# A hybrid S5 and HGRN2 block on one core: the framework orders three engines by another machine model, and two raw weight tiles change their pool

## The chip, the cores and the metric

The kernel runs on one core of one Trainium2 chip. The metric is the device time of one execution in microseconds, as a median of three runs. A profiled execution has a time of its own; its span, from the first to the last instruction on the engines, is a little shorter. The engines are TensorE (PE in the profile's rows; PEld is its loading of weights), VectorE (DVE), ScalarE (ACT) and GpSimd (POOL). SyncE (SP) computes nothing here and issues most of the DMAs; ScalarE issues some too.

## The reference

The block takes x (2048 tokens of width 1024, float32), normalises it, projects it to nine pieces, sends them through two causal token mixers, merges the two with gates, projects once more, adds x and normalises again. Cut to what matters:

```python
xn = rms_norm(h, norm_w)
proj = xn @ w_in                                   # 1024 -> 5632
u_a, z_a, q_b, f_b, i_b, og_b, z_b, g_a, g_b = split(proj)
y_a = s5_branch(u_a, z_a, ...)                     # diagonal complex state space, GELU, GLU, gate
y_b = hgrn2_branch(q_b, f_b, i_b, og_b, z_b, ...)  # gated linear recurrence, head norm, gate
merged = sigmoid(g_a) * (y_a @ w_proj_a) + sigmoid(g_b) * (y_b @ w_proj_b)
out = rms_norm(h + merged @ w_out, final_norm_w)
```

## The kernel before

**Tiling.** The sequence is cut into two halves of 1024 tokens (index `a` in names), each half into two blocks of 512 (index `b`). All products have 512 columns and use operands split into a high and a low part in the format fp32r: `split` (lines 118 to 120) copies the high part on ScalarE (L119) and subtracts on VectorE to get the low part (L120), and each product is three matmuls, high by high, high by low, low by high. The input projection is cut into 22 slices of 256 output columns. The first slices (u, the first q/f and the first i/og) are multiplied plainly for the first half (`plain`, L355 to L357). All others go through `strassen` (L458 to L460), which forms seven products in place of eight; the sums of the results are ScalarE copies and VectorE additions (L464, L467), and the weight operands come from `w_ops`.

**Weights.** For the first half `w_ops` loads a slice's raw weights (L383), splits them, forms the seven operands and stores them to DRAM (L391, tensors `wc`). For the second half it reads them back (L375). Four slices of the second half were plain in the first: numbers 0 and 1 (u), 2 (the first q/f, `SL_QF`) and 6 (the first i/og, `SL_VO`). For these the raw weights are loaded once more. Which pool they go to is what line 382 decides: `y4` has two buffers of 128x1024, `wr4` has three.

**The mixers.** The HGRN2 core (`hgrn_block`) runs nine levels of score products (L959 to L991, tiles `sc`), each with VectorE updates of Q and K between them (L1016, L1017), then the state (L1029, L1038) and the output. Its root mean square is the accumulated square of L1054, a Newton iteration on VectorE (L155 to L161, tile `rso`), a scaled ScalarE copy (L1077, tile `ys`) and a transpose on TensorE (L1081). The S5 core (`ssm_batch`) has VectorE work around three products (L791, L829, L830). `norm_stats` loads x (L186, L190, tiles `xr`) and accumulates its squares on ScalarE (L187, L191); `norm_diag` and `norm_bcast` turn them into factors by way of one product with ones (L205). `x_load` reads the transformed second half of x back (L287, tiles `xq`, also from the pool `y4`) and splits it into the tiles `X1..`, which names write as X103h for half 1, row block 0, operand 3, high part.

**What sets the order.** TensorE's order is written by hand: the whole body stands in a block in which the order of the code is TensorE's, and lists of timed events (`heads`, `steps`, `timed`) place the mixers' steps between the matmuls of the projection. The order of the other engines and of the DMA queues is not the code's. The framework's scheduler walks the program with a model of the machine, and whenever an engine is free in that model it gives it, among the instructions that are ready in the model, the one that stands first in the code. Each engine then runs its list strictly in that order on the chip, and a tile's buffer is given out in that order too. The lines that matter here:

```python
yp = ctx.enter_context(tc.tile_pool(name="yp", bufs=2))          # y4
wpool = ctx.enter_context(tc.tile_pool(name="wpool", bufs=3))    # wr4
...
raw = (y4 if a and sl != SL_VO else wr4)(f"rw{n}_{kh}")...
...
with tc.manual_schedule(engines={mybir.EngineType.PE}):
...
with tile.TileContext(nc) as tc:
```

Of the kernel before, what the change touches and what calls it, by code (L numbers as in the profile page):

```python
# [27 lines left out]
SL_U, SL_QF, SL_VO, SL_ZB, SL_ZA, SL_GA, SL_GB = 0, 2, 6, 10, 12, 14, 18  # L28
# [3 lines left out]
def hybrid_block(  # L32
# [24 lines left out]
    nc = tc.nc  # L57
# [48 lines left out]
    def wo4(name):  # L106
        return wpool.tile([128, 1024], F32R, name=name, tag="wo", bufs=5)
# [10 lines left out]
    def split(raw, hi, lo):  # L118
        S.activation(hi, raw, AF.Copy)  # L119
        V.tensor_tensor(lo, raw, hi.bitcast(F32), op=ALU.subtract)  # L120
# [249 lines left out]
    def w_ops(a, sl):  # L370
        n = f"{a}_{sl}"
        if sl in wc_d:
            for p in range(7):
                t = wo4(f"w{n}_{p}")
                nc.sync.dma_start(t.bitcast(F32), wc_d[sl][p])  # L375
                yield t
            return
        if a == 0:
            wc_d[sl] = [dram.tile([128, 1024], F32, name=f"wc{sl}_{p}") for p in range(7)]

        def get(kh):
            raw = (y4 if a and sl != SL_VO else wr4)(f"rw{n}_{kh}").rearrange("p (k n) -> p k n", k=4)
            nc.sync.dma_start(raw, wi[sl, kh])  # L383
            return raw[:, :, 0:128], raw[:, :, 128:256]

        def op(p, raw):
            t = wo4(f"w{n}_{p}")
            v = t.rearrange("p (i k n) -> p i k n", i=2, k=4)
            split(raw, v[:, 0], v[:, 1])
            if a == 0:  # L390
                nc.sync.dma_start(wc_d[sl][p], t.bitcast(F32))  # L391
            return t

        a11, a21 = get(0)
        yield op(0, a11)
        a12, a22 = get(1)
        s1 = wpool.tile([128, 4, 128], F32, name=f"s1{n}", tag="wt", bufs=2)
        s2_ = wpool.tile([128, 4, 128], F32, name=f"s2{n}", tag="wt", bufs=2)
        t = op(1, a12)
        V.tensor_tensor(s1, a21, a22, op=ALU.add)  # L400
        yield t
        V.tensor_tensor(s2_, a11, s1, op=ALU.subtract)
        yield op(2, s2_)
        t = op(3, s1)
        V.tensor_tensor(a11, a11, a21, op=ALU.subtract)
        yield t
        t = op(4, a11)
        V.tensor_tensor(a12, a12, s2_, op=ALU.add)
        yield t
        yield op(5, a22)  # L410
        yield op(6, a12)
# [1232 lines left out]
```

## Time and profile before

| | us |
|---|---|
| median of three runs (1541.31 to 1543.61) | 1541.35 |
| the profiled execution | 1540.05 |
| its span | 1538.3 |
| TensorE busy | 1467.0 |
| TensorE loading weights | 1207.3 |
| VectorE busy | 1100.8 |
| ScalarE busy | 637.6 |
| TensorE's waits of over 0.2 us, together | 63 |

Busy times overlap between engines, so they do not add up. TensorE is busy 95% of the span. The granted clock stands at full speed nearly throughout; ten short stretches are at half speed, the last of them at the end.

### The profile page before, as it was taken

What the parts mean: (1) busy time and instruction counts of PE and PEld (TensorE: products, weight loads), DVE (VectorE), ACT (ScalarE), POOL (GpSimd) and SP (SyncE); (2) the same over time, 40 slices, a digit from 0 to 9 for tenths busy, and PEclk for the clock granted to TensorE, in tenths of its full rate; (3) what the DMA queues carried; (4) which work ended last, traced back from release to release, by engine and by line L of the source; (5) the groups of instructions that cost most, each with busy time, mean ns of one, the idle gap of its engine ahead of it and who ended that gap; (6) DMA issues with size and microseconds to landing.
All of it is one profiled execution on the core that took longest, in us unless ns stands there. A gap on an engine that the chain in (4) does not pass through costs nothing.

```text
span 1538.3 us, 21386 instructions
## 1 busy us (share of the span) xinstructions
PE 1467.0 (95%) x7360; PEld 1207.3 (78%) x7360; DVE 1100.8 (72%) x2409; ACT 637.6 (41%) x1391; POOL 3.6 (0%) x24
## 2 busy tenths in 40 slices
PE   7997999999999999999989999999989899899997
PEld 5776788788888777878878887788878688688886
DVE  5798688678678659956665887776649877765445
ACT  7456454454454634323323455333353332532222
POOL 0000000000000000000000000000000000000000
PEclk9998999999999999999999999999999999999999
DMA  9539778977977883786668559677977854854602
GB/s 336 175 115 305 284 278 295 316 255 269 331 264 286 285 271 119 186 245 197 231 201 313 174 163 294 217 259 264 327 236 234 266 184 137 274 171 131 212 14 103
DMA packets 192060, 354.53 MB, mean 230 GB/s; under 512 B 65680, under 2 KB 74896, under 8 KB 191952
## 3 DMA queue, kind: packets, MB, share of 16 engines
q1 hardware_dynamic: 163792, 328.00, 63.6%
q10 hardware_dynamic: 28160, 25.17, 4.8%
q8 instruction: 58, 0.95, 0.3%
q14 instruction: 50, 0.41, 0.1%
HBM read 214.17 MB, written 138.94 MB: 230 GB/s over the span
## 4 chain that ended last, share of the span: by engine, by line
PE 68%; DVE 15%; DMA 10%; ACT 3%; issue 3%; SPq 0%; ACTq 0%; DVEq 0%
PE pd L458 14%; PE pd L460 13%; PE pd L459 13%; PE pf L1284 3%; PE pf L1285 3%; PE pf L1286 3%; PE pp L1112 2%; PE pp L1111 2%; PE pp L1110 2%; PE sc L979 2%; DMA y_d<-T 1%; DVE w L120 1%; DMA xb<-in_xt_dram 1%; DMA xq<-xo_d 1%; PE pd L355 1%
## 5 line engine op out<-in xcount | busy, mean ns | idle before, releaser
L119 ACT ACTIVATE w<-rw 128x512 fp32r<-128x512 f32 x110 | 68.7, 628 | 112.7 <-PE pd L460 67.9
L1284 PE MATMUL pf<-ho,mh 128*128 128x512 f32 x256 | 101.2, 395 | 5.2 <-ACT mh L119 5.2
L1286 PE MATMUL pf<-ho,ml 128*128 128x512 f32 x256 | 100.6, 393 | 0.5 <-DVE ml L120 0.5
L1285 PE MATMUL pf<-lo,mh 128*128 128x512 f32 x256 | 100.3, 392 | 0.0
L464 ACT ACTIVATE u<-pd 128x512 f32<-128x512 f32 x80 | 47.5, 594 | 106.0 <-PE pd L460 103.3
L120 DVE TENSOR_TENSOR w<-rw,w 128x512 fp32r<-128x512 f32 x110 | 75.3, 685 | 16.9 <-ACT w L119 16.6
L467 DVE TENSOR_TENSOR u<-u,pd 128x512 f32<-128x512 f32 x80 | 54.8, 685 | 33.5 <-PE pd L460 22.8
L355 PE MATMUL pd<-xh,hw 128*128 128x512 f32 x128 | 52.4, 409 | 9.0 <-ACT hw L119 6.7
L1284 PEld LDWEIGHTS pf<-ho,mh 128*128 128x128 f32 x256 | 48.6, 190 | 15.4 <-ACT mh L119 5.5
L1286 PEld LDWEIGHTS pf<-ho,ml 128*128 128x128 f32 x256 | 48.4, 189 | 11.6 <-DVE ml L120 1.6
L1285 PEld LDWEIGHTS pf<-lo,mh 128*128 128x128 f32 x256 | 48.6, 190 | 9.9
L119 ACT ACTIVATE mh<-sgl 128x512 fp32r<-128x512 f32 x32 | 20.0, 629 | 86.7 <-DVE sgl L1227 86.3
L356 PE MATMUL pd<-xl,hw 128*128 128x512 f32 x128 | 51.2, 400 | 0.0
L357 PE MATMUL pd<-xh,lw 128*128 128x512 f32 x128 | 50.9, 397 | 0.0
L980 DVE COPY_PREDICATED s_buf<-masks,sc 128x256 f32<-128x256 uint8 x64 | 32.5, 508 | 25.0 <-PE sc L979 25.0
L1110 PE MATMUL pp<-yh,hpa 128*128 128x512 f32 x128 | 50.2, 392 | 0.0
L1112 PE MATMUL pp<-yh,lpa 128*128 128x512 f32 x128 | 49.9, 390 | 0.2 <-DVE lpa L120 0.2
L1111 PE MATMUL pp<-yl,hpa 128*128 128x512 f32 x128 | 50.0, 390 | 0.0
L1226 DVE TENSOR_TENSOR sgl<-sgl,pp 128x512 f32<-128x512 f32 x48 | 32.7, 683 | 23.0 <-PE pp L1112 22.9
L1016 DVE TENSOR_TENSOR Q<-Q,t 128x256 f32<-128x256 f32 x96 | 40.5, 422 | 10.0 <-PE sc L991 9.9
L974 ACT ACTIVATE KX<-K 128x128 f32<-128x128 f32 x128 | 32.6, 304 | 35.6 <-DVE K L1017 26.3
L979 PEld LDWEIGHTS sc<-Q,KX 128*128 128x128 f32 x256 | 38.0, 189 | 8.9 <-issue 1.8
(915 smaller groups left out, 4431.6 us busy)
## 6 DMA issues: line engine op xcount, KB each, us to landing
wc<-w SPq DMA_DIRECT2D x126, 512.0 KB, 3.4
w<-wc SPq DMA_DIRECT2D x126, 512.0 KB, 4.6
rw<-in_wi_dram SPq DMA_DIRECT2D x44, 512.0 KB, 4.6
sgl<-sg_d SPq DMA_DIRECT2D x48, 256.0 KB, 3.2
sg_d<-u ACTq DMA_DIRECT2D x32, 256.0 KB, 3.5
ro<-in_wo_dram SPq DMA_DIRECT2D x16, 512.0 KB, 5.1
hh<-in_xn_dram SPq DMA_DIRECT2D x32, 256.0 KB, 5.1
out_dram<-hh SPq DMA_DIRECT2D x32, 256.0 KB, 2.4
```

The lines of the kernel that those rows point to most:

```text
L119: S.activation(hi, raw, AF.Copy)
L120: V.tensor_tensor(lo, raw, hi.bitcast(F32), op=ALU.subtract)
L458: mm(o, w[:, 0, k], xh, start=(first and k == 0), stop=False, skip_group_check=True)
L459: mm(o, w[:, 0, k], xl, start=False, stop=False, skip_group_check=True)
L460: mm(o, w[:, 1, k], xh, start=False, stop=(k == 3), skip_group_check=True)
L979: mm(ps[:, :, c, :], ch(kx, c), qp, start=True, stop=True)
L1110: mm(ps, hi[:, k, fs], yh, start=(k == 0), stop=False)
L1111: mm(ps, hi[:, k, fs], yl, start=False, stop=False)
L1112: mm(ps, lo[:, k, fs], yh, start=False, stop=(k == last))
L1284: mm(o, mh[:, ts_], hi, start=(kk == 0), stop=False)
L1285: mm(o, mh[:, ts_], lo, start=False, stop=False)
L1286: mm(o, ml[:, ts_], hi, start=False, stop=(kk == 7))
```

## The change

Two edits. The scheduler is told to use its timeline model in place of the default one while it orders VectorE, ScalarE and the queues. And the raw weights of slice 2 of the second half, which is the first slice of that half, are loaded into `wr4` and no longer into `y4`; slices 0 and 1 stay in `y4`, slice 6 stays in `wr4`.

```diff
-            raw = (y4 if a and sl != SL_VO else wr4)(f"rw{n}_{kh}").rearrange("p (k n) -> p k n", k=4)
+            raw = (y4 if a and sl < SL_QF else wr4)(f"rw{n}_{kh}").rearrange("p (k n) -> p k n", k=4)
...
-    with tile.TileContext(nc) as tc:
+    with tile.TileContext(nc, schedule_with_timeline_sim=True) as tc:
```

No instruction is added or removed. TensorE's list is the same, row for row. VectorE's list of some 2300 rows differs from end to end, ScalarE's and SyncE's lists in most stretches. Three places are shown; the names carry the tile's indices.

ScalarE in the first half, while slice 10 (the first z slice) is multiplied. `u20_10` and `u30_10` are copies of a product out of `pd0_10_0`, after which TensorE may write that bank again; `xr..` are loads of x for the second half's norm, squared here. Before:

```order
L191 ACTIVATE xr102_1268,ssx_237<-xr102_1268 128x1024
L191 ACTIVATE xr103_1271,ssx_237<-xr103_1271 128x1024
L974 ACTIVATE KX001_1357<-K001_1355 128x64x2 x2
L464 ACTIVATE u20_10_1316<-pd0_10_0_1224 128x512
L191 ACTIVATE xr110_1505,ssx_237<-xr110_1505 128x1024
L191 ACTIVATE xr111_1508,ssx_237<-xr111_1508 128x1024
L464 ACTIVATE u30_10_1391<-pd0_10_0_1224 128x512
```

The same place in the changed kernel:

```order
L191 ACTIVATE xr102_1268,ssx_237<-xr102_1268 128x1024
L119 ACTIVATE w0_14_1_1413<-rw0_14_1_1409 128x512
L191 ACTIVATE xr103_1271,ssx_237<-xr103_1271 128x1024
L191 ACTIVATE xr110_1505,ssx_237<-xr110_1505 128x1024
L464 ACTIVATE u20_10_1316<-pd0_10_0_1224 128x512
L191 ACTIVATE xr111_1508,ssx_237<-xr111_1508 128x1024
L191 ACTIVATE xr112_1511,ssx_237<-xr112_1511 128x1024
L191 ACTIVATE xr113_1514,ssx_237<-xr113_1514 128x1024
L464 ACTIVATE u30_10_1391<-pd0_10_0_1224 128x512
```

One square has moved ahead of `u20_10`, and two more ahead of `u30_10`.

ScalarE at the end of the first half's projection. `ys030` is the scaled copy that the transpose L1081 reads, `Y031h` the high part of the last head's output, which `merge_b` multiplies (L1110, L1111); the tiles X1.. are splits of loads by `x_load`. Before:

```order
L1077 ACTIVATE ys030_5298<-O030_4557,rso_240 128x128 x4
L1077 ACTIVATE ys031_5343<-O031_4512,rso_240 128x128 x4
L119 ACTIVATE Y030h_5325<-zy030_4987 128x512
L119 ACTIVATE X132h_5453<-xq21_5391 128x512
L119 ACTIVATE X103h_5476<-xq30_5419 128x512
L119 ACTIVATE X113h_5501<-xq30_5419 128x512
L119 ACTIVATE Y031h_5370<-zy031_4989 128x512
L119 ACTIVATE X123h_5526<-xq31_5457 128x512
L119 ACTIVATE X133h_5549<-xq31_5457 128x512
L119 ACTIVATE X104h_5572<-xq40_5505 128x512
```

The same place in the changed kernel:

```order
L119 ACTIVATE X103h_5476<-xq30_5419 128x512
L1077 ACTIVATE ys030_5298<-O030_4557,rso_240 128x128 x4
L1077 ACTIVATE ys031_5343<-O031_4512,rso_240 128x128 x4
L119 ACTIVATE X113h_5501<-xq30_5419 128x512
L119 ACTIVATE Y030h_5325<-zy030_4987 128x512
L119 ACTIVATE X123h_5526<-xq31_5457 128x512
L119 ACTIVATE X133h_5549<-xq31_5457 128x512
L119 ACTIVATE X104h_5572<-xq40_5505 128x512
L119 ACTIVATE Y031h_5370<-zy031_4989 128x512
```

The split X103h, which needs the load xq30, has moved ahead of `ys030`; three splits of the loads xq31 and xq40 have moved ahead of `Y031h`.

SyncE's queue in the second half, where slice 15's stored operand 4 (`w1_15_4`, L375) is read back among the loads for the first S5 batch (WU00, VM00, E0). Before:

```order
L375 DMA w1_15_3_7557<-wc15_3_2410 128x1024
L863 DMA zb_d1_2_176<-ezb121_7572 128x512
L758 DMA WU00_7585<-w_d_87 128x512
L759 DMA WU00_7585<-u_d0_0_92 128x512
L760 DMA VM00_7586<-v_d_88 128x512
L761 DMA VM00_7586<-m_d_89 128x512
L767 DMA E0_7594<-el_d_90 128x4x32
L768 DMA E0_7594<-eh_d_91 128x4x16
L375 DMA w1_15_4_7597<-wc15_4_2411 128x1024
```

The same place in the changed kernel:

```order
L375 DMA w1_15_3_7557<-wc15_3_2410 128x1024
L767 DMA E0_7594<-el_d_90 128x4x32
L768 DMA E0_7594<-eh_d_91 128x4x16
L375 DMA w1_15_4_7597<-wc15_4_2411 128x1024
L383 DMA rw1_0_0_8321<-in_wi_dram 128x1024
L863 DMA zb_d1_3_177<-ezb130_7534 128x512
L375 DMA w1_19_0_7654<-wc19_0_2653 128x1024
L782 DMA cs_d0_108<-CC00_7591 128x512
L375 DMA w1_15_5_7681<-wc15_5_2412 128x1024
```

The read of operand 4 now stands ahead of four loads of the S5 batch and of the store that it followed.

## Rows read from the trace of the kernel before

**Rows 1.** The page: the span, and TensorE's busy time, its share and its instructions.

```profile
span 1538.3 us, 21386 instructions
PE 1467.0 (95%) x7360; PEld 1207.3 (78%) x7360; DVE 1100.8 (72%) x2409; ACT 637.6 (41%) x1391; POOL 3.6 (0%) x24
```

**Rows 2.** What TensorE waited for, longest first: the waiting line, what ended the wait, then us in total, times, the longest. The view has 22 such rows, from the first to the last shown here; a row for the first weights (6.7 us at the start of the program) is among those left out.

```profile
PE pd L458 <- ACT u L464: 13.4, 4, 6.6
...
PE pg L1110 <- ACT gh L119: 6.7, 2, 3.9
...
PE pf L1284 <- ACT mh L119: 5.2, 1, 5.2
PE pd L458 <- DMA w<-wc: 4.5, 2, 2.6
PE sc L967 <- DVE kl L120: 4.5, 1, 4.5
PE pv L1029 <- DVE st L1038: 3.4, 2, 2.0
...
PE sc L979 <- DVE Q L1016: 2.2, 2, 1.4
...
PE pp L1112 <- DVE lpa L120: 0.2, 1, 0.2
```

**Rows 3.** The start. One row of busy times by stretch (us from:to, length, busy us and count of TensorE, weight loads, VectorE, ScalarE, GpSimd, then granted clock, DMA share, GB/s), then rows of the timeline (start us, us, engine, line, operation, count): the loads of x for the first norm, the last square, the last step of the factors, and the two products with ones.

```profile
0.00:38.00 38.00, 28.97 (x110) 22.49 (x111) 21.45 (x46) 27.57 (x55) 2.04 (x10) 1.00 0.95 337
```

```profile
13.95 5.06 SPq L186 DMA_DIRECT2D xr<-in_xn_dram  x8
24.10 0.63 ACT L187 ACTIVATE xr<-xr 128x512 f32<-128x512 f32 x1
30.21 0.88 DVE L200 TENSOR_SCALAR dg<-ident,rst 128x128 f32<-128x128 f32 x4
31.85 1.02 PE L205 MATMUL psn<-dg,ones 128*128 128x512 f32 x2
55.70 1.13 PE L205 MATMUL psn<-dg,ones 128*128 128x512 f32 x2 [1.03 <-DVE dg L200]
```

**Rows 4.** The timeline of ScalarE and TensorE around the first place shown above: `u20_10` (L464), the squares of xr110 and xr113 (L191), and the two matmuls that write over what `u20_10` and `u30_10` copied; then the time from issue to landing of the eight loads of these tiles.

```profile
130.69 0.57 ACT L464 ACTIVATE u<-pd 128x512 f32<-128x512 f32 x1
134.24 1.06 ACT L191 ACTIVATE xr<-xr 128x1024 f32<-128x1024 f32 x1 [2.97 <-DMA xr<-in_xn_dram]
141.31 1.05 ACT L191 ACTIVATE xr<-xr 128x1024 f32<-128x1024 f32 x1
131.32 0.80 PE L458 MATMUL pd<-X004h,w 128*128 128x512 f32 x1 [6.60 <-ACT u L464]
139.28 0.39 PE L458 MATMUL pd<-X005h,w 128*128 128x512 f32 x1
DMA to landing us min/median/max: 3.8/4.7/7.3
```

**Rows 5.** The timeline near 230 us: the VectorE addition that makes `u30_7`, the first two scalings of the next block of x, and the transpose that reads `u30_7`.

```profile
229.49 0.68 DVE L467 TENSOR_TENSOR u<-u,pd 128x512 f32<-128x512 f32 x1
236.90 1.41 DVE L248 SCALAR_TENSOR_TENSOR xa<-xa,nw_t,rb 128x512 f32<-128x512 f32 x2 [0.77 <-DMA xa<-in_xt_dram]
230.89 0.60 PE L911 MATMUL pt<-ident,u 128*128 128x128 f32 x4
```

**Rows 6.** The timeline around the second place: `ys030` and `ys031`, X103h, `Y031h`, X104h on ScalarE, and the matmul that reads the low part of `Y031`.

```profile
540.33 2.43 ACT L1077 ACTIVATE ys<-O,rso 128x128 f32<-128x128 f32 x8
543.93 0.62 ACT L119 ACTIVATE X103h<-xq 128x512 fp32r<-128x512 f32 x1
548.86 0.63 ACT L119 ACTIVATE Y031h<-zy 128x512 fp32r<-128x512 f32 x1 [3.79 <-DVE zy L1082]
550.44 0.61 ACT L119 ACTIVATE X104h<-xq 128x512 fp32r<-128x512 f32 x1
550.88 0.50 PE L1111 MATMUL pb<-Y031l,hpb 128*128 128x512 f32 x1 [0.84 <-DVE Y031l L120]
```

**Rows 7.** SyncE's queue at the third place: the last load of the S5 batch ahead of operand 4, and the read of operand 4 (L375).

```profile
784.03 0.59 SPq L768 DMA_DIRECT2D E<-eh_d  x1
786.56 0.33 SPq L375 DMA_DIRECT2D w<-wc  x1
```

**Rows 8.** The price of one VectorE operation on 128x512 (the costliest group of the page: busy us, mean ns), and the timeline near 1109 us: the last Newton step of `rso`, the copy `ys130` that needs it, and the transpose that needs the copy.

```profile
L120 DVE TENSOR_TENSOR w<-rw,w 128x512 fp32r<-128x512 f32 x110 | 75.3, 685 | 16.9 <-ACT w L119 16.6
```

```profile
1108.42 0.17 DVE L161 SCALAR_TENSOR_TENSOR rso<-small,rso 128x8 f32<-128x8 f32 x1
1108.67 1.28 ACT L1077 ACTIVATE ys<-O,rso 128x128 f32<-128x128 f32 x4 [0.40 <-DVE rso L161]
1109.12 0.33 PE L1081 MATMUL py<-ident,ys 128*128 128x128 f32 x1 [1.31 <-ACT ys L1077]
```

**Rows 9.** The timeline near 1219 us: the low part of `mh006`, and the matmul of the output projection that reads it.

```profile
1218.76 0.68 DVE L120 TENSOR_TENSOR ml<-sgl,mh 128x512 fp32r<-128x512 f32 x1
1219.49 0.49 PE L1286 MATMUL pf<-ho,ml 128*128 128x512 f32 x1 [0.32 <-DVE ml L120]
```

**Rows 10.** Busy times by stretch, as in the first row of Rows 3: the four microseconds behind a wait of 1.9 us near 804 us, and eleven behind the wait of 5.2 us near 1225 us.

```profile
804.00:808.00 4.00, 3.60 (x9) 2.89 (x10) 3.04 (x6) 0.00 (x0) 0.10 (x1) 0.57 0.53 176
...
1224.00:1235.00 11.00, 8.74 (x28) 6.98 (x29) 10.03 (x20) 4.28 (x9) 0.00 (x0) 0.53 0.83 265
```

## The prediction

> **What bounds the kernel now.** I read the page's first lines, then TensorE's waits, then the timeline around each of them. The page shows TensorE busy 1467 of 1538 us [rows 1]. The 22 rows of its waits come to 63 us, the longest single ones 6.7, 6.6 and 5.2 [rows 2]: that sum, less the 6.7 us for the first weights, is all that a better order can take out directly. Behind a wait the granted clock can fall to the lower of its two levels: 0.57 for four microseconds after 804 us, 0.53 for eleven after 1224 us, which cost 1.7 and 5.2 us [rows 10]. Nearly every wait ends on ScalarE or VectorE, so what matters is what stands ahead of a product that TensorE needs, on an engine that works strictly down its list.
>
> **How I price a moved row.** TensorE's list does not change, so I keep its matmuls where the trace has them, go down the changed list of the other engine from the last row that is tied to a matmul or a landing, and add the traced durations; if the product comes out later than its matmul started, the difference is added. Where a wait of before finds its product earlier, the difference is taken off. One 128x512 VectorE operation costs 0.685 us [rows 8].
>
> **Start.** In SyncE's queue ten DMAs (four loads of x of 0.26 MB, three raw weight loads of 0.26, two masks of 0.36, one tiny) move ahead of the eight xr loads of the first norm: 2.55 MB. The DMA engines are 0.95 busy in this stretch at 337 GB/s, so they cost 7.6 us [rows 3]. The last square, at 24.1, would come at about 31.7; of the 5.5 us from its end to the end of the factors, 30.21+0.88, some 3.0 us were four x splits that are now done before. So the first product with ones, which started unhindered at 31.85, starts near 35: +3.5 (0 to 4.4, the nearest rows being no displacement and all 7.6). The second product's factors do not come later, so its wait of 1.0 goes, -0.9. **Term 1: +2.6.** The Trainium skill, DMA: Bandwidth & Descriptors, section Rules for kernel authors, says to issue a DMA early and wait late, since its fixed cost is then hidden. By that rule the move is free and the total would be 2.6 lower; the DMA share of 0.95 is why I don't follow it here [rows 3].
>
> **105 to 165 us.** The wait for kl (4.5) and one of 0.6 go, since HGRN2 rows move up on VectorE. But on ScalarE `u20_10` now stands behind the square of xr110, which ran at 134.24 after waiting for its load. It then ends at 134.24+1.06+0.57 = 135.9, and the matmul that waited for it until 131.32 is 4.6 late [rows 4]. `u30_10` stands behind the square of xr113: 141.31+1.05+0.58 = 142.9 at the earliest, two squares that now come between push it to 144.1, and its matmul at 139.28 is 4.9 late, 0.3 beyond the first [rows 4]. These times already contain the waits that go. Bounds: had xr110's load taken the shortest 3.8 us in place of the longest 7.3, the first would be 1.1 [rows 4]; if all of term 1 shifts the loads too, terms 1 and 2 add fully. **Terms 1 and 2 together: between 4.9 and 7.5, I take +6.2.** Behind the square stand the low-part copies and score levels of two HGRN2 blocks, and TensorE waits for those as well; they are late by less than 5 us each, so they add nothing of their own.
>
> **Near 230 us.** Three scalings of x (L248, 0.7 us each) move ahead of the addition for `u30_7`, which ended at 230.17 for a matmul at 230.89 [rows 5]: 2.1-0.7 = 1.4 late. **Term 3: +1.4** (0 if VectorE has caught up; 4 if the raw weights behind which it also stands land 3 us later, as their load moves down by that much).
>
> **306 us.** The state update behind which TensorE waited moves ahead of two scalings: one of the two pv waits, 2.0 of the 3.4, goes [rows 2]. **Term 4: -2.0.**
>
> **520 to 552 us.** `ys030`, at 540.33, now stands behind X103h, which ran at 543.93: a delay between 0 and 3.6+0.6; xq loads take some 6 us from issue, which puts it at 2.2. `Y031h` stands behind X104h, so ends no earlier than 550.44+0.61+0.63 = 551.7, its low part 0.7 later at 552.4, for a matmul at 550.88: 1.5 [rows 6]. Since Y031 follows from the transposes of `ys`, the two add. **Term 5: +3.7** (0 to 5.7).
>
> **580 to 600 us, the pool edit.** The raw weights of slice 2 no longer hold the two `y4` buffers, so the xq loads and the weights can come earlier. No wait of over 0.3 us stands there in the waits view, so earlier is worth nothing: 0. What hides it is a TensorE that is fully busy; if the wr buffers came late in turn, three of them are shared with the projection weights of `merge_b`, which are all loaded by then.
>
> **667 to 672 and 790 to 805 us.** The Q updates of level 5 move up: both waits, 2.2, go. The read of operand 4, issued at 786.56 and waited for, moves ahead of four S5 loads and is done long before; operand 6 likewise: 4.5 [rows 2, 7]. **Term 6: -6.7.**
>
> **1109 us.** The Newton steps for `ys130` end at 1108.42+0.17. On the changed list three low-part splits stand between the steps, of 0.685 each, and the S5 rows that stood behind: 3.0 later, less a little, at 1111.4. The matmul is 2.8 later [rows 8]. **Term 7: +2.8.** Seven more places between 613 and 1170 us have the same form, one to three VectorE operations of 0.685 moved ahead of a product with no slack: by full count 7 x 2 x 0.685 = 9.6, by none 0. **Term 8: +7.0**, nearer the full count, as such a queue starts at a matmul a few us earlier and moves along with TensorE.
>
> **1215 to 1236 us.** The wait for mh, 5.2 [rows 2], falls to 0.6, and one of 0.9 behind it goes. The low part `ml` gets five operations more ahead of it, 3.4, with 0.1 of slack: +3.1 [rows 8, 9]. One S5 load gets a buffer that is free only after the preceding S5 product: +1.8. **Term 9: -0.6.** **1329 to 1346 us.** The waits for gh, 6.7 [rows 2], fall by 3.2 with their low parts' 0.6, and three operations ahead of another low part add 2.2. **Term 10: -1.5.**
>
> **Sum.** 6.2+1.4-2.0+3.7-6.7+2.8+7.0-0.6-1.5 = +10.3. The half-speed stretch at 804 goes (-1.7); new waits of 2 us or more near 32, 231, 540 and 1109 can each bring one of 1.7; I count the clock as 0, between -7 and +7. The profiled execution took 1540.05, so 1550.4; the median of the runs shown stands 1.3 above it: 1551.7, or 1552.
>
> **Rivals.** *Catch-up, faster.* A late TensorE gives VectorE, busy 72%, time to work off its list, so that delays in a stretch do not add. Then of terms 3, 7 and 8 nothing is left (-11.2), and with the two half-speed stretches that follow removed waits gone (-6.9) the time is 1534. It decides if VectorE is idle for over a microsecond shortly before such a product. For it: that 72%. Against: the late products hang on matmuls of the same stretch, which move too. *Loads land early, no change.* If the loads in the new order land at the short end, terms 1, 2 and 5 go: 1552-9.9 = 1542. Against: the DMA share of 0.95 at the start. *All adds up, slower still.* The upper ends of terms 1 to 3, 5 and 8 are +1.3, +2.6, +2.0 and +2.6, the clock +7: 1567. The zero fills of `m_d` (L699), which move from all over the first half into a burst before 235 us, point that way. *The model changes little.* The lists could differ only in rows with slack; then gains and losses are each a few us, 1541. The rows above speak against it.
>
> **Chances.** Forecast with 1545 to 1560: 0.42. Slower still: 0.20. Catch-up: 0.25. The two without change: 0.13. About 0.2%, 3 us, is what a measurement of this kernel can tell from no change, so slower (above 1544.4) has 0.62, within 0.13, faster (below 1538.3) 0.25. The range reaches from below the faster rival to above the slowest: 1529 to 1573; the likeliest case's own is 1545 to 1560.
>
> **What would show it.** TensorE's waits should show new rows for the product with ones near 35 us, for `u` at L464 with a longer first wait, for `ys` near 545 and 1112, for `ml` near 1220; the rows for w from wc, for kl and for mh should be gone or short. TensorE's busy time should stay within a few us of 1467. I am wrong if the waits come to less than 60 us in all, above all if the first place near 131 us has a wait of no more than 6.6.

## The result and the profile after

The changed kernel takes **1562.87 us** (median of 4 runs, 1560.43 to 1565.34) against 1541.33 of the kernel before on the same chip: a ratio of 1.0138, interval 1.0114 to 1.0162, so 21.5 us slower. The prediction said 1552, slower, with a range of 1529 to 1573. The sign and this outer range hold. The range of its likeliest case, 1545 to 1560, was missed, and the loss is twice the one worked out, +21.5 in place of +10.3.

The page's first lines of the changed kernel, to be read beside [rows 1]:

```profile
span 1558.6 us, 21427 instructions
PE 1472.3 (94%) x7360; PEld 1210.4 (78%) x7360; DVE 1098.0 (70%) x2409; ACT 636.8 (41%) x1391; POOL 4.2 (0%) x24
```

The span grew by 20.3. TensorE is busy 5.3 us longer with the same matmuls: that is the clock. VectorE and ScalarE do the same work as before. (The 41 more instructions in the first line are semaphore waits, which are not counted as busy; the computing engines have the same counts.) So 15 us must be waits. The waits of TensorE, as in [rows 2] (line, what ended the wait, us in total, times, longest); 24 rows, 78 us in all against 63:

```profile
PE pd L458 <- ACT u L464: 19.8, 4, 14.5
PE pt L911 <- DVE u L467: 9.9, 3, 5.9
PE py L1081 <- ACT ys L1077: 8.2, 3, 5.1
...
PE pd L460 <- DVE w L120: 3.4, 1, 3.4
PE psn L205 <- DVE small L169: 3.2, 1, 3.2
...
PE psg L791 <- DMA WU<-u_d: 1.8, 1, 1.8
...
PE pf L1286 <- DVE ml L120: 1.1, 2, 0.9
...
PE pd L458 <- DMA w<-wc: 0.7, 1, 0.7
PE pf L1284 <- ACT mh L119: 0.7, 1, 0.7
```

Gone or short, as forecast: kl (4.5), mh (5.2), w from wc (4.5 to 0.7). New or longer, as forecast: the product with ones (L205), u at L464 (longest 6.6 to 14.5), ys near 1129 (but not near 545, see below), ml. Far beyond the forecast: u at L467, 9.9 us, 5.9 of it in one wait. Not on its list: w at L460, 3.4.

**By place.** TensorE's rows are the same in both kernels, so each matmul's start after, less its start before, is a lag; how much it grows in a stage is what the stage costs, waits and clock together. Beside it the prediction's terms, by stage (us of the kernel before), and in the last column what TensorE's waits alone grew by; the rest of the lag is longer busy time of the same matmuls, 5.3 in all:

| stage | terms | predicted | lag grew by | of it waits |
|---|---|---|---|---|
| 0 to 187 | 1, 2 | +6.2 | +8.6 | +8.4 |
| 187 to 492 | 3, 4 | -0.6 | +6.4 | +4.6 |
| 492 to 700 | 5, part of 6 | +1.5 | -0.1 | -0.6 |
| 700 to 834 | rest of 6 | -4.5 | -5.6 | -3.9 |
| 834 to 1021 | 7, 8 together | +9.8 | +5.5 | +4.0 |
| 1021 to 1173 | (with the row above) | | +10.5 | +6.4 |
| 1173 to 1254 | 9 | -0.6 | -3.3 | -2.0 |
| 1254 to the end | 10 | -1.5 | -2.0 | -2.1 |
| sum | | +10.3 | +20.0 | +14.8 |

The start: one row by stretch as in [rows 3], then the loads of x for the first norm on SP, and the product with ones. The loads are issued from 20.60, before from 13.95; the product starts 3.8 later.

```profile
0.00:38.00 38.00, 25.83 (x93) 19.62 (x94) 23.07 (x61) 24.76 (x45) 2.04 (x10) 1.00 0.93 327
```

```profile
20.60 5.12 SPq L186 DMA_DIRECT2D xr<-in_xn_dram  x8
35.66 1.10 PE L205 MATMUL psn<-dg,ones 128*128 128x512 f32 x2 [3.19 <-DVE small L169]
```

The first place, as in [rows 4]: the squares of xr103 and xr110 on ScalarE, the first after 4.14 us of waiting for its load, then `u20_10`, then the matmul.

```profile
136.37 1.06 ACT L191 ACTIVATE xr<-xr 128x1024 f32<-128x1024 f32 x1 [4.14 <-DMA xr<-in_xn_dram]
137.42 1.04 ACT L191 ACTIVATE xr<-xr 128x1024 f32<-128x1024 f32 x1
138.46 0.57 ACT L464 ACTIVATE u<-pd 128x512 f32<-128x512 f32 x1
139.09 0.80 PE L458 MATMUL pd<-X004h,w 128*128 128x512 f32 x1 [14.51 <-ACT u L464]
```

Near 230 us, as in [rows 5]. First the zero fills of `m_d` on SP as a group (issue ns min/median/max, first and last start), of the kernel before:

```profile
L699 SPq DMA_DIRECT2D m_d<-zt x28: 423/445/1954, 198.6 to 432.8; - x28
```

and of the changed kernel:

```profile
L699 SPq DMA_DIRECT2D m_d<-zt x28: 303/440/1973, 207.1 to 238.2; - x28
```

The same 28 issues of 0.44 us now stand within 31 us. Then, from the changed kernel's timeline: two runs of fills, the issue of the raw weights rw0_11_1, VectorE's row that needs them, the addition for `u30_7`, and the transposes that read it.

```profile
214.70 3.23 SPq L699 DMA_DIRECT2D m_d<-zt  x6
...
219.84 2.74 SPq L699 DMA_DIRECT2D m_d<-zt  x6
...
231.49 0.42 SPq L383 DMA_DIRECT2D rw<-in_wi_dram  x1
```

```profile
238.21 0.69 DVE L400 TENSOR_TENSOR s<-rw,rw 128x512 f32<-128x512 f32 x1 [6.05 <-DMA rw<-in_wi_dram]
...
245.43 0.68 DVE L467 TENSOR_TENSOR u<-u,pd 128x512 f32<-128x512 f32 x1
```

```profile
246.16 1.11 PE L911 MATMUL pt<-ident,u 128*128 128x128 f32 x4 [5.92 <-DVE u L467]
```

Before, rw0_11_1 was issued at 219.74 and L400 ran at 225.08. Now VectorE stands idle for 6.05 us with the addition for `u30_7` queued behind.

The second place, as in [rows 6]: X103h now stands ahead of `ys`, X104h ahead of `Y031h`, and both wait for loads.

```profile
555.66 0.63 ACT L119 ACTIVATE X103h<-xq 128x512 fp32r<-128x512 f32 x1 [1.25 <-DMA xq<-xo_d]
556.20 2.44 ACT L1077 ACTIVATE ys<-O,rso 128x128 f32<-128x128 f32 x8
...
563.96 0.63 ACT L119 ACTIVATE X104h<-xq 128x512 fp32r<-128x512 f32 x1 [3.24 <-DMA xq<-xo_d]
564.49 0.61 ACT L119 ACTIVATE Y031h<-zy 128x512 fp32r<-128x512 f32 x1
```

VectorE's last Newton step for `ys030` ended at 555.39, so X103h held the copy back by 0.8 us. TensorE came late itself, and its wait there is shorter than the 2.3 us of before:

```profile
556.63 0.33 PE L1081 MATMUL py<-ident,ys 128*128 128x128 f32 x1 [0.59 <-ACT ys L1077]
```

Near 1129, as in [rows 8]: VectorE's last Newton step, ScalarE from there, and the transposes.

```profile
1128.72 0.17 DVE L161 SCALAR_TENSOR_TENSOR rso<-small,rso 128x8 f32<-128x8 f32 x1
```

```profile
1124.28 0.63 ACT L874 ACTIVATE u<-u 128x512 f32<-128x512 f32 x1 [0.24 <-DVE u L467]
...
1128.92 2.44 ACT L1077 ACTIVATE ys<-O,rso 128x128 f32<-128x128 f32 x8 [3.02 <-DVE rso L161]
```

```profile
1129.38 1.35 PE L1081 MATMUL py<-ident,ys 128*128 128x128 f32 x4 [5.11 <-ACT ys L1077]
```

The clock, as in [rows 10]: three stretches at the lower level (0.50), each around a wait; and the eleven microseconds from 1224, at 0.53 before, now full.

```profile
129.70:143.40 13.70, 4.31 (x10) 3.45 (x11) 6.09 (x21) 5.18 (x11) 0.00 (x0) 0.50 0.78 295
242.30:249.10 6.80, 2.94 (x9) 2.55 (x10) 6.80 (x14) 1.79 (x5) 0.00 (x0) 0.50 1.01 373
...
1224.00:1235.00 11.00, 11.00 (x59) 9.38 (x58) 9.34 (x16) 4.41 (x9) 0.00 (x0) 1.00 0.91 305
1245.80:1252.60 6.80, 5.50 (x17) 4.07 (x18) 6.80 (x13) 2.31 (x4) 0.00 (x0) 0.50 1.05 389
```

### The profile page after: what moved, and what is told of

Same layout as the page of the kernel before. It is cut to its first block, busy times and chain, and to the rows that moved or that the text cites. A ratio compares the mean times of both kernels' runs of the same rounds, so it can differ in the third digit from the quotient of the medians.

```text
span 1558.6 us, 21427 instructions
## 1 busy us (share of the span) xinstructions
PE 1472.3 (94%) x7360; PEld 1210.4 (78%) x7360; DVE 1098.0 (70%) x2409; ACT 636.8 (41%) x1391; POOL 4.2 (0%) x24
## 4 chain that ended last, share of the span: by engine, by line
PE 61%; DMA 9%; DVE 9%; ACT 3%; issue 2%; SPq 1%; ACTq 0%; DVEq 0%
PE pd L458 12%; PE pd L460 12%; PE pd L459 12%; PE pf L1286 2%; PE pf L1285 2%; PE pf L1284 2%; PE pp L1111 2%; PE pp L1112 2%; PE pp L1110 2%; DMA yy<-y_d 1%; PE sc L979 1%; DMA y_d<-T 1%; DMA xq<-xo_d 1%; PE pt L911 1%; ACT ya L844 1%
## 5 line engine op out<-in xcount | busy, mean ns | idle before, releaser
L464 ACT ACTIVATE u<-pd 128x512 f32<-128x512 f32 x80 | 47.6, 595 | 116.8 <-PE pd L460 115.5
L467 DVE TENSOR_TENSOR u<-u,pd 128x512 f32<-128x512 f32 x80 | 54.6, 682 | 33.1 <-PE pd L460 26.5
L1110 PE MATMUL pp<-yh,hpa 128*128 128x512 f32 x128 | 51.0, 398 | 0.8 <-ACT yh L119 0.8
L1111 PE MATMUL pp<-yl,hpa 128*128 128x512 f32 x128 | 50.5, 394 | 1.3 <-DVE yl L120 1.3
L1292 ACT ACTIVATE pf<-hh 128x512 f32<-128x512 f32 x32 | 19.2, 600 | 59.2 <-DVE hh L1290 59.2
```

What stands on the lines that cost most here:

```text
L467: V.tensor_tensor(z[key], z[key], ps, op=ALU.add)
L1110: mm(ps, hi[:, k, fs], yh, start=(k == 0), stop=False)
L1111: mm(ps, hi[:, k, fs], yl, start=False, stop=False)
```

## The experiments

The theory after the result: the order alone makes the loss, in stages that add, and in each of them a row that waits for a transfer stands ahead of one that TensorE needs. Rivals: the pool edit; catch-up, so that losses of one stage vanish in the next; late loads that limit a stage whatever the order of the rows. Ratios are to the kernel before on the same chip. In the experiments on the order, each row of an engine's list is tied to the row ahead of it without a wait, so that the list in the kernel fixes the order of VectorE, ScalarE and SP:

```diff
         hybrid_block(tc, *args)
+        _row(tc, ROW_DVE)
+        _row(tc, ROW_Activation)
+        _row(tc, ROW_SP)
```

**Which edit.** Two runs, each with one of the two edits undone in the changed kernel. The flag alone:

```diff
-            raw = (y4 if a and sl < SL_QF else wr4)(f"rw{n}_{kh}").rearrange("p (k n) -> p k n", k=4)
+            raw = (y4 if a and sl != SL_VO else wr4)(f"rw{n}_{kh}").rearrange("p (k n) -> p k n", k=4)
```

> Only the scheduler's flag is changed; the raw weights of slice 2 stay in the two y4 buffers. If the order alone makes the loss, the ratio to before is 1.010 to 1.017 (16 to 26 us more), as with both edits. Rival: the pool edit carries a good part of the loss; then this is at most 1.007 (11 us).

The pool edit alone:

```diff
-    with tile.TileContext(nc, schedule_with_timeline_sim=True) as tc:
+    with tile.TileContext(nc) as tc:
```

> Only the pool of slice 2's raw weights is changed, with the default order. If the pool edit is free by itself: within 0.2% of before (3 us). Rival, that it carries a part of the loss: 5 us or more above before.

Measured: the flag alone 1559.93 us, 1.0119 [1.0096, 1.0142]; the pool edit alone 1540.88, 1.0001 [0.9986, 1.0016]. The order makes the loss, the pool edit costs nothing, as forecast.

**Do the stages add?** The kernel before, with the lists of the changed one put in by stage (by the changed kernel's time: 1 to 195 us, 2 to 507, 3 to 715, 4 to 843, 5 to 1036, 6 to 1198, 7 to 1276, 8 to 1385):

```diff
+    order of stages 1 and 2, or 5 and 6, or 4, 7 and 8: rows of the kernel after
     order of all other stages: rows of the kernel before
```

> The kernel before, with the changed kernel's order on VectorE, ScalarE and SyncE in the first two stages only (0 to 507 us of the changed kernel's trace), where TensorE's lag rose by 8.6 and 6.4 us; before's order and before's pools afterwards. If losses stay lost: 15 us more than before, ratio 1.0097. Rival, catch-up: the waits that before has later (on weights from DRAM near 790 to 805, on Q near 670, on mh, gh) shrink since the other engines had time to get ahead of a late TensorE; then 5 to 9 us more, and its trace has those waits short although the order there is before's.

> The kernel before, with the changed kernel's order in two stages only (843 to 1198 us), in which TensorE's lag rose by 5.5 and 10.5 us. If places add: 16 us more than before, ratio 1.0104, 1557. Rival, catch-up in later stages: at most 6 us more.

> The kernel before, with the changed kernel's order on VectorE, ScalarE and SyncE in three stages only (715 to 843, 1198 to 1276 and 1276 to 1385 us of the changed kernel's trace), in which TensorE's lag fell by 5.6, 3.3 and 2.0 us; before's order everywhere else. If what a stage does to the time is its own (places add): 10.9 us less than before, ratio 0.993, 1530. Rival, catch-up: the gains are only TensorE working off waits that earlier stages had brought; then the time is within 3 us of before.

Measured: stages 1 and 2 1557.82, 1.0105 [1.0081, 1.0129]; stages 5 and 6 1556.04, 1.0102 [1.0079, 1.0126]; stages 4, 7 and 8 1538.92, 0.9988 [0.9971, 1.0004]. The losses come in full, alone, and nothing behind them is caught up. The gains do not come with the stages in which they appeared: 0.12% in place of 0.7%. One more run asked whether they need stage 3:

> The rows of VectorE, ScalarE and SP in the order of the kernel before from 0 to 507 us and from 843 to 1198 us, and in that of the kernel after in the stages 507 to 843 and 1198 to 1385 us, with the weight buffers of the kernel after. In the trace of the kernel after these four stages gave TensorE back 0.1, 5.6, 3.3 and 2.0 us, 11 in all; with the order of 715 to 843 and 1198 to 1385 us alone only 2 came. Theory (the 5.6 us of 715 to 843 need the loads that stage 507 to 715 issues earlier): with both stages they come, 1529 to 1534 us, a ratio of 0.991 to 0.996, and the waits for w near 792 and 804 us are under 1 us each. Rival (they are only what a TensorE that is 14 us late gets back at those loads, which come when they come): 1537 to 1542 us, a ratio of 0.998 to 1.001, and the waits for w stay over 1.5 us each.

Measured: **1530.66, 0.9931 [0.9908, 0.9954]**. They do. Stages 3 and 4 give 2.7 and 5.8 us in its trace. The reason stands in SP's row: the read of w1_15_6 and the one behind it, ahead of the matmul that waits, without stage 3 (stages 4, 7, 8 alone):

```profile
799.34 0.81 SPq L375 DMA_DIRECT2D w<-wc  x2
```

```profile
803.17 0.76 PE L458 MATMUL pd<-X106h,w 128*128 128x512 f32 x1 [2.71 <-DMA w<-wc]
```

and with stage 3:

```profile
789.50 0.89 SPq L375 DMA_DIRECT2D w<-wc  x2
```

SP's list is the same at this place, but without stage 3 what stands ahead of the reads (stores of `w_d` and `m_d` that wait for VectorE and earlier transfers) gets through 10 us later, though TensorE itself is only 4 us later at the end of stage 3, and TensorE waits; with stage 3 no wait for w is left. The three parts are the whole of the order but for a few rows behind 1385 us, and they add: +1.05% and +1.02% less 0.69% is 1.38%, the ratio of the changed kernel. The sum is known to some 0.4% by the three intervals, so that it fits to the last digit is chance.

**Stage 2: the fills.** The changed kernel with 21 of the 28 fills spread again, and VectorE's row that needs them all (dd0, L742) moved back to where it stood. Without that move the rows wait for each other in a circle, and the run that left it out, k4_fills_spread, has no time.

```diff
 SP, 207 to 238 us
-L699 m_d<-zt  (runs of up to 6)
+L699 m_d<-zt  (one behind every second later transfer)
```

> The kernel after with 21 of the 28 zero fills of m_d (line 699) taken out of their burst on SP and put one behind every second later transfer, and with nothing else moved but the read-out of d0 that waited on them. Theory: the burst, at 0.42 to 0.5 us of issue each, made the load of rw0_11_1 late (issued 231.49 us against 219.74 before, landed 238.19 against 224.00), and the row that waits for it stood ahead of the addition of u30_7; without the burst the 5.92 us wait at 246 shrinks to under 1 us and with it one half-clock stretch goes, so 5 to 8 us fewer than the kernel after: a ratio to the kernel before of 1.0085 to 1.0105. Rival: the low parts and scalings that stand ahead of u30_7 make it late by themselves, and the wait stays over 3 us: a ratio of 1.0125 or more.

Measured: 1551.47, 1.0069 [1.0042, 1.0097], some 11 us less than the changed kernel by the ratios, 9.1 by the spans, which is more than the 5 to 8 expected. Stage 2 costs nothing any more (lag -0.9 in place of +6.4), which is 7.2 of the 9.1; the rest is spread over later stages, with both signs. Its trace, VectorE's row that needs rw0_11_1, the addition for `u30_7` and the transposes:

```profile
232.44 0.68 DVE L400 TENSOR_TENSOR s<-rw,rw 128x512 f32<-128x512 f32 x1
...
239.65 0.68 DVE L467 TENSOR_TENSOR u<-u,pd 128x512 f32<-128x512 f32 x1
```

```profile
240.44 0.60 PE L911 MATMUL pt<-ident,u 128*128 128x128 f32 x4
```

No wait stands there, with the scalings still ahead: alone, they cost nothing, and without the burst the loss of this stage is gone. With the burst they may add to it. From L400 to the addition it is 7.2 us here as in the changed kernel, and 4.4 before; a run with the burst and without the scalings was not made.

The page DMA: Bandwidth & Descriptors of the Trainium skill, section Issuing engines are not separate DMA queues, says that the issue of a DMA is usually short beside the DMA itself. One fill agrees: 0.44 us of issue, 3.2 us to landing. Of what many issues on one queue add up to, the sentence says nothing. In SP's list 8 fills stand ahead of rw0_11_1 before and 24 after, and 16 times 0.44 is 7.0 us for the load behind them. Measured, with the fills spread it is issued at 225.74 and lands at 231.80, with the burst at 231.49 and 238.19: 5.8 and 6.4 us.

**Stage 1: the copies and the norm.** The changed kernel with `u20_10` and `u30_10` ahead on ScalarE; dg10 and dg11 take another ring of buffers, so that u20_10's buffer does not depend on the squares:

```diff
-        dg = sn(f"dg{a}{b}")
+        dg = s2(f"dg{a}{b}") if a else sn(f"dg{a}{b}")
 ScalarE
+L464 u20_10<-pd0_10_0
 L119 kh000<-KX000
...
 L119 w0_14_1<-rw0_14_1
+L464 u30_10<-pd0_10_0
 L191 xr103,ssx<-xr103
 L191 xr110,ssx<-xr110
-L464 u20_10<-pd0_10_0
...
 L191 xr113,ssx<-xr113
-L464 u30_10<-pd0_10_0
```

> The changed kernel with its own order, except that on ScalarE the two copies u20_10 and u30_10 stand ahead of the squares whose loads they waited behind; the product dg10, dg11 of the norm takes its buffer from another ring, without which the copy could not move. If the squares ahead of the copies make the loss near 131 to 148 us: the waits of 14.5 and 0.5 us go, with some 5 us of half-speed clock behind them, of which up to 7 come back as the wait for kl and for weights that this stall had covered: 8 to 15 us less than the changed kernel, ratio to before 1.004 to 1.009. Rival, the loads themselves are the limit (what TensorE does next waits for them too): less than 4 us are gained, ratio 1.011 or more.

Measured: 1560.36, 1.0118 [1.0094, 1.0142], as the rival has it. The 14.5 us wait at 139 is gone. In its place, VectorE's Newton step that needs the last square, and the matmul behind it:

```profile
149.81 0.17 DVE L155 TENSOR_SCALAR small<-ssx 128x4 f32<-128x4 f32 x1 [6.51 <-ACT xr L191]
```

```profile
151.06 1.22 PE L979 MATMUL sc<-Q,KX 128*128 128x128 f32 x4 [11.02 <-DVE s_buf L960]
```

So on top of that edit the norm's rows were put behind too:

```diff
 VectorE
-L155 to L161, L200 (norm 10)     ahead of L960 s_buf
+L155 to L161, L200 (norm 10)     behind L120 w0_14_3
-L155 to L161, L200 (norm 11)
+L155 to L161, L200 (norm 11)     behind L120 w0_14_6
 ScalarE
-L191 squares of xr103 to xr113   ahead of L119 w0_14_2
+L191 squares of xr103 to xr113   behind L119 w0_14_2, L974 KX and L119 w0_14_3
```

> The kernel after with u20_10's and u30_10's copies ahead as in k3_u_copies_ahead, and on top of it the rows that wait for the chain of xr loads put behind those that TensorE needs: on VectorE both blocks of Newton steps and dg scalings behind the low parts w0_14_3 and w0_14_6, on ScalarE the squares of xr103 to xr113 behind w0_14_2, KX and w0_14_3. Theory (the loss at 131 to 160 us comes from rows that wait for a landing ahead of rows that TensorE needs): the waits of 3.50 us at 136 and 11.02 us at 151 of k3_u_copies_ahead fall under 3 us together and two half-clock stretches go; 8 to 14 us fewer than the kernel after, a ratio of 1.0045 to 1.0085. Rival (the loads themselves limit this stage: whatever stands first, the weights and scores behind the same loads are as late): the waits move on to another matmul of the same 40 us, a ratio of 1.011 or more.

Measured: 1562.55, 1.0130 [1.0101, 1.0159]; the rival. Both waits went (lag -6.8 at 135 us), and by 160 us all was back: waits of 2.7, 2.6 and 3.3 us, and VectorE idle for the next late load, the raw weights rw0_18_1:

```profile
162.08 0.69 DVE L400 TENSOR_TENSOR s<-rw,rw 128x512 f32<-128x512 f32 x1 [7.47 <-DMA rw<-in_wi_dram]
```

In this stage the loads bind, not the rows that happen to wait for them first. rw0_18_1 is issued at 157.01 in the changed kernel and at 145.97 before. For the first late load, xr103, SP's list shows what has changed: between the load of xr102 and it stand five more transfers, two of them raw weights, where before stood none, and it is issued 4.3 us later (127.84 against 123.51) and lands 6.9 later. Which of SP's rows would have to move was not tried, so that this order makes the 8.6 us of the stage is likely and not shown.

The kernel before met the same limit. Its own order, with rows moved by hand at its longest waits but those for kl and for the first weights:

```diff
 VectorE, ScalarE, SP of the kernel before
+L464 u20_10, u30_10 ahead of the squares; both norms behind L120 w0_14_3, w0_14_6
+L464, L467 u31_21 ahead of the rows of yy10 (L844) and gz (L1183)
+L1226, L1227, L119 of mh007 and the rows of T14 ahead of those of yy11
+L1178 gy102, gy112 ahead of the output writes L1318
```

> The kernel before, its own order, with rows moved by hand at four places: u20_10's and u30_10's copies ahead of the squares, and the Newton steps of both norms behind the low parts (118 to 160 us; wait of 6.60 us at 131 and two half-clock stretches); u31_21's copy and addition ahead of the rows of yy10 that wait for its load (5.64 us at 1135, two stretches); in the pair of scan and output projection the rows of mh007, ml007 and T14 ahead of those of yy11 (5.22 and 0.88 us at 1225, three stretches); the reads of gy102 and gy112 ahead of the output writes on SP (3.87 and 2.83 us at 1329 and 1345, two stretches). Theory (at each place a row that waits for a landing stands ahead of one that TensorE needs): half to all of 24 us of waits and about 13 us of half clock come off, 1505 to 1525 us, a ratio of 0.977 to 0.990. Rival (as with the order of stages 4, 7 and 8, what comes off at a place is given back at the next late load): 1533 to 1541 us, a ratio of 0.995 to 1.000.

Measured: 1540.72, 0.9999 [0.9981, 1.0017]; the rival. The waits of 6.6, 5.6 and 5.2 us fell to 0.7 or less, that of 3.9 to 1.3, and the time went into the next rows that wait for loads:

```profile
150.92 0.69 DVE L400 TENSOR_TENSOR s<-rw,rw 128x512 f32<-128x512 f32 x1 [3.25 <-DMA rw<-in_wi_dram]
```

```profile
158.74 0.68 PE L979 MATMUL sc<-Q,KX 128*128 128x128 f32 x4 [2.88 <-DVE Q L1016]
...
1236.15 2.05 PE L791 MATMUL psg<-WU 128*128 128x128 f32 x8 [4.80 <-DMA WU<-u_d]
```

**Stages 5 and 6.** First the Newton steps of ys120 and ys130 put on end on VectorE, as term 7 has them as the cause:

```diff
 VectorE
-L156 to L161 among L797, L808, L813, L815, L816, L120
+L156 to L161, one behind the other, right behind L155
```

> The changed kernel with its own order, except that on VectorE the steps of two Newton iterations (for ys120 and ys130) stand together and no longer alternate with S5 rows and low-part splits. If the rows between the steps make the waits of 2.5 us near 993 and 5.1 near 1129: both fall to below 1.5, and 5 to 8 us are gained with the clock, ratio 1.009 to 1.0105. Rival, give-back: the next wait in line (for u31_21, 4.6 us near 1155, behind a load) grows by as much, and less than 3 us are gained.

Measured: 1562.09, 1.0128 [1.0106, 1.0150], no measurable gain, as the rival has it. The steps end 7 us earlier; `ys130` does not start earlier:

```profile
1121.66 0.17 DVE L161 SCALAR_TENSOR_TENSOR rso<-small,rso 128x8 f32<-128x8 f32 x1
```

```profile
1127.43 0.63 ACT L874 ACTIVATE u<-u 128x512 f32<-128x512 f32 x1 [2.22 <-DVE u L467]
...
1128.96 2.44 ACT L1077 ACTIVATE ys<-O,rso 128x128 f32<-128x128 f32 x8
```

On ScalarE the SiLU of u31_17 (L874) stands ahead and waits for an addition on VectorE that stands behind the scan rows. In the changed kernel that SiLU is through at 1124.91 and the Newton steps are the last to come; put on end, they push the addition from 1123.56 to 1126.71 (1.2 of it is that this run stands later there as a whole), and the SiLU with it. So the run moves the delay from one VectorE product to another and does not clear the steps. Then, in the kernel with the fills spread, the scalings of `ys` were moved ahead of it as well, and u31_21 ahead of yy10:

```diff
 VectorE: Newton steps on end as above; L467 u31_21 ahead of L847 yy10
 ScalarE
+L1077 ys120, ys121     ahead of L464 u31_5
+L1077 ys130, ys131     ahead of L464 u31_17
-L1077 ys130, ys131     behind L874 u31_17 and L464 s11_21
+L464 u31_21            ahead of L844 ya10<-yy10
```

> The kernel k4b_fills_spread (the order after, its fills spread) with rows moved at the places of its longest waits between 984 and 1155 us: the Newton steps for ys120 and ys130 on end on VectorE, the scalings of ys120, ys121, ys130 and ys131 on ScalarE ahead of the copies and SiLUs of u31_5 and u31_17 (which wait for additions that stand behind scan rows on VectorE), and u31_21's copy and addition ahead of the rows of yy10 that wait for its load. Theory (in stage 1036 to 1198 the loss is made by such rows standing ahead on ScalarE; in k5_newton_together the Newton steps were done 7 us before ys130's scaling began): the waits of 2.51, 5.09 and 4.86 us at 985, 1123 and 1149 us fall under 3 us together and two half-clock stretches go, 7 to 12 us fewer than k4b_fills_spread, a ratio to the kernel before of 0.999 to 1.0025. Rival (as at 131 us: what comes off goes into the next load that lands no earlier, that of yy10 and the gy tiles): a ratio of 1.005 or more, with new waits of over 6 us together between 1125 and 1240 us.

Measured: 1545.68, 1.0040 [1.0023, 1.0057], between the two. The span is 8.1 us below that with the fills spread alone, the ratio 4.5 us below, with intervals that overlap. The waits for ys are gone (2.5 and 5.1 us) and that for u31_21 fell from 4.9 to 0.7; 3.3 and 2.1 us came back at 1139 and 1156. The first of them is again such a row, which this edit had left ahead of the addition:

```profile
1135.93 0.69 DVE L1183 TENSOR_TENSOR gz<-gz,gy 128x512 f32<-128x512 f32 x1 [11.59 <-DMA gy<-ya_d]
...
1137.85 0.68 DVE L467 TENSOR_TENSOR u<-u,pd 128x512 f32<-128x512 f32 x1
```

```profile
1138.58 0.50 PE L458 MATMUL pd<-X106h,w 128*128 128x512 f32 x1 [3.34 <-DVE u L467]
```

## Why the prediction was right, and where its size was off

**The frame held.** The span is TensorE's work plus its waits; what moved is seen in the waits, 63 to 78 us, and the pool edit is free. The sum goes by stages, and the measured parts add to the whole within what the runs can tell. That the time lies in the outer range says little: it was drawn from below the faster rival to above the slowest. What came is *slower still*, which had a chance of 0.20. The 10 us that the sum lacks are the clock, 5.3 and counted as 0, and some 5 us of waits in the stage of term 3. The misses of the other terms run from -2.1 to +2.2 a stage and cancel to about -1, which is luck.

**Terms 1 and 2, +6.2.** The lag at the product with ones is 3.8 (3.5 said) and falls to 2.7 with the second one (term 1: 2.6 said). By the rule of the Trainium skill cited there (DMA: Bandwidth & Descriptors, section Rules for kernel authors), as the prediction reads it, this product would have started on time. The trace went with the DMA share. At 131 us the mechanism is the one named, `u20_10` behind xr110's square; the lag behind it is 7.8, and 8.6 at the end of the stage, above the bound of 7.5. The missing part: term 2 placed the square by the landing of before, and the loads of xr103 and xr110 landed 6.9 and 3.1 later (136.0 and 137.3). And the 3.4 us wait for w at L460 was not on the list. The two repairs show that the landing is the cause that counts: without `u20_10` behind the squares the stage is no shorter.

**Term 3, +1.4: the step that failed.** It priced three scalings of x, with 4 as the bound if the raw weights landed 3 us late. They landed 14 us later than before (238.19 against 224.00), some 8 of it because the whole stage came late, 6.4 by the fills that had moved ahead of them on SP. The lag grew by 7.5 at this place, 5.9 of it the wait and 1.6 the clock, and the fills spread give back 9 to 11 us in all. The prediction named the burst in the rival *All adds up*, without a price, though SP's list gave it: 16 more issues ahead of the load, 7.0 us.

**Terms 4 to 6.** Term 4, -2.0: 1.9 came, by a wait that vanished. Term 5, +3.7: the lag grew by 2.2 between 520 and 556 us, and not as told. X103h held `ys030` back by 0.8 (2.2 said), and a wait for the HGRN2 state (L1046, 2.3 us), which no term had, made TensorE late before it, so the wait at `ys030` fell from 2.3 to 0.6. At `Y031` the waits grew by 1.4 (1.5 said). Term 6, -6.7: about 7 by the trace, of which 5.2 are waits. But its place was told wrongly: reading operand 4 and 6 earlier in SP's list gives nothing by itself (0.9988 with the order of that stage and of 7 and 8); it takes the order of the stage before, by which SP reaches these rows earlier.

**Terms 7 and 8, +9.8.** Measured +16.0 over both stages. Of it 10.4 are waits, so the sum of the places came out; 5.7 is TensorE's longer busy time, with 24 us at the lower clock in place of 10. The form is right (a product behind rows that were moved ahead). By single places the agreement is partly luck. At ys130 the wait grew by 3.8 (2.8 said), since four low-part splits ran between the Newton steps and not three. The wait for `u` near 1021 grew from 1.1 to 2.9, behind a VectorE row that itself waits, while 0.685 us a row is the price of rows that run. That for u31_21 fell by 1.1.

**Terms 9 and 10, -2.1.** Measured -5.3, of which -4.1 are waits: the load of WU cost the 1.8 foreseen, but the wait for `ml` is 0.9 at its longest, not 3.1.

**The clock, 0.** It cost 5.3 by TensorE's busy time, within the +-7 given: ten stretches became thirteen, 48 us at the lower level became 74, and the one around the wait at 139 is 13.7 us long, though only 4.3 us of matmuls fall in it. Most of the cost, 4.1, lies between 1021 and 1173 us.

**The rivals.** *Catch-up* is refuted as an account of the whole: stages 1 and 2 alone lose 1.05%, 5 and 6 alone 1.02%, with nothing given back behind; at single places (`ys030`) it is what happened. *Loads land early* went the other way: they land later, since more is issued ahead of them. *All adds up* was closest, 1567 against 1562.87; it had the right reasons for term 3 and for the clock.

**Slips in the working.** From the end of the last square to the end of the factors it is 6.4 us, not 5.5, which ends at the start of their last step [rows 3]; with it the first product would be some 0.9 later, and the measured 3.8 lies between. Without term 1 the joint +6.2 would fall to 4.9, so the total would be 1.3 lower and not 2.6. And 1.7 and 5.2 us for the half-speed stretches take TensorE as busy all through them; it was for 3.60 of 4.00 and 8.74 of 11.00 us [rows 10].

**What stays open.** Shown by runs are the order as the cause, the stages that add, and the fills. In stage 1 the loads limit, but what makes them late was not tried. Of the 16 us of stages 5 and 6, moved rows gave back 4.5 by the ratios and 8.1 by the spans; where the rest comes from is read from traces alone.

**A version that beats both.** The changed kernel's order from 507 to 843 us and from 1198 to 1385, with its pools, and the order of before elsewhere: 1530.66 us, 0.9931 [0.9908, 0.9954].

## What to carry to other kernels

Price a moved row on the queue that issues transfers as well as on the engines: count the issues that now stand ahead of each load that somebody waits for, by the issue time in the trace. Moving a product ahead of the row that blocks it is worth little where the next row waits for a load that is just as late: four runs that did only that gained nothing that could be measured, a fifth gained 4.5 us by ratios whose intervals overlap, and the one that moved transfers (and one VectorE row with them) gained about 10 us. An order that loses as a whole can hold stretches that win: put in by stage, their effects added here within what the runs can tell, some 0.4%, but a gain shown in one stage had its cause in the stage before.

## What the runs showed of the hardware

A zero fill of `m_d` took 0.44 us of SP's time to issue (median; up to 2.0), more than a 0.26 MB load of x for the norm (median 0.33): the issue is not cheaper for a small transfer.

Loads that had 3.8 to 7.3 us from issue to landing before [rows 4] took 3.6 to 8.2 in the changed kernel. The slowest of them and the fastest, each from issue to landing, in rows as in [rows 3]:

```profile
127.84:136.01 8.17, 0.00 (x0) 0.00 (x0) 3.67 (x6) 2.54 (x5) 0.00 (x0) 0.61 1.03 419
137.54:141.15 3.61, 2.06 (x5) 1.68 (x6) 2.85 (x16) 1.49 (x3) 0.00 (x0) 0.50 0.63 188
```

The slow load was under way while the DMA engines were full, the fast one while they were not. The share of 0.78 in the row from 129.70 is a mean over both.

Around the 14.5 us wait the granted clock fell to the lower level (1.2 GHz) 9 us before the wait ended and rose again 4.3 us after it. The wait of 6 us at 246 brought one of 6.8 us in the same way.
